# A hybrid decoder layer on one core: the learned tokens' values in one product, and the recurrence's weights rounded behind an eviction

## The chip, the cores and the metric

The kernel runs on one core of a Trainium2 chip. The metric is the device time of one execution in microseconds (us) on the slowest core, which here is the only one. The times are medians of several runs on the chip; the profile shows one further execution.

## The reference, cut to what matters

The layer takes 1024 tokens of width 1024, puts 16 learned tokens ahead of them, and computes a SwiGLU block, a mixer of two parallel head groups, and a second SwiGLU block, all in float32:

```
h = h + 1/2 * swiglu_1(rms_norm(h))
u = rms_norm(h) @ w_in            # one projection for both head groups
o = concat(hgrn2(u_hgrn), stick_breaking(u_sb))
h = h + o @ w_out
h = h + 1/2 * swiglu_2(rms_norm(h))

# recurrence, 4 heads of 128 x 128
S_t = diag(f_t) S_(t-1) + (1 - f_t) v_t^T ;  o_t = S_t^T q_t
# attention, 8 heads of width 64, strictly causal, z = q.k / sqrt(64)
A[t,s] = sigmoid(z_ts) * prod over s<j<t of (1 - sigmoid(z_tj)) ;  o = A v
```

The columns s of A run over the 16 learned tokens too. The change touches the product A v for those 16 columns, and the weights of the recurrence's part of w_in.

## The kernel before, in words

A float32 product on TensorE (PE) is made of three matmuls of rounded parts: each operand is split into an upper part (rounded to the type fp32r, "hi") and a lower part (what is left, "lo"), and hi·hi, lo·hi and hi·lo are added up in a PSUM bank (`product`, L251 to L261; the matmuls are L258, L259 and L260). A column of 128 outputs of w_in takes 24 such matmuls for every piece of up to 512 tokens.

The weights of such a column come through `split_w` (L224). One DMA on the queue of SyncE (SP) loads 128x1024 numbers (`raw`, two buffers, L236). ScalarE (ACT) rounds them (`wh`, a cast, L241), and VectorE (DVE) subtracts (`wl`, L243); `wh` and `wl` have three buffers each.

The first SwiGLU block ends a little before 700 us. Then come the projections of the attention (until about 840 us). For every pair of heads `sb_v` (L1432) brings the values into rows per token: DVE transposes 32x32 blocks (`vt`), ACT and DVE split them (`vhl`), and SP stores them into a buffer in DRAM, vD (L1454), from which a head's values come back as one tile v of 128 rows, 9 groups and 128 columns (64 upper parts, 64 lower parts, L1531). Group 0 holds the 16 learned tokens, in 16 of its 128 rows; the other rows are filled with zeros by 16 DMAs (L1598). The 16 learned tokens' part is handled last in each pair.

The recurrence needs 16 columns of w_in: v, f, q and g for each of its four heads (`hgrn_fill`, L1127). `part` (L1168) makes one half of one piece of a column. A column's first call loads and splits the weights of the column after it. A piece that is finished is emptied from its bank by `use`: for v by one copy on ACT (L1144), for f by two sigmoids on ACT (L1150, L1151) with two products on DVE (L1152, L1155), and for q and g by a sigmoid on ACT (L1158) and a product on DVE (L1159). v and f have four pieces of 256 or 264 tokens, q and g two of 512.

From about 862 to 1142 us a braid runs: PE's order is written out by hand and alternates the attention's jobs with halves of the recurrence's columns. A job takes 256 queries of a head. Scores (`z`, L1649 to L1652, two banks) go through two sigmoids on ACT (keep L1655, sig L1656) that leave the bank free, a running product on DVE (L1659), and a product on GpSimd (POOL, L1665). PE then transposes the weights ("flip", L1504 for four blocks of 128 keys, L1558 for the learned tokens; two banks). `sb_parts` (L1625) splits what was flipped: ACT rounds (L1627), DVE subtracts (L1628), into the tiles wu, or wm for the learned tokens, and the bank is free. PE multiplies with the values (`values`): L1579 takes all 128 columns of v with the upper part of the weights, L1581 the 64 upper columns of v with the lower part. So the learned tokens cost two matmuls per job, each over 128 rows of which 16 hold something.

The instructions of ACT, DVE, GpSimd and SP are put into an order by the framework's scheduler ahead of the run, and each of these engines then takes its instructions strictly in that order. `issue_after` tells the scheduler to place an instruction behind another one.

Of the kernel before, what the change touches and what calls it, by code (L numbers as in the profile page):

```python
# [49 lines left out]
class Block:  # L50
# [172 lines left out]

    def split_w(self, view, parts=None):  # L224
        nc = self.nc
        n = int(np.prod(view.shape[1:]))
        if parts is not None:
            got = []
            for i, tag in enumerate(self.w_tags):
                t = self.wp.tile([P, n], F32R, tag=tag, name="w" + "hl"[i], bufs=self.w_bufs)  # L230
                self.last_load = nc.sync.dma_start(t.bitcast(F32), parts[:, i])
                got.append(t)
            return got
        raw = self.wp.tile([P, n], F32, tag="raw", name="raw", bufs=self.raw_bufs)
        to = raw.rearrange("p (k f) -> p k f", k=view.shape[1]) if len(view.shape) == 3 else raw
        self.last_load = nc.sync.dma_start(to, view)  # L236
        hi = self.wp.tile([P, n], F32R, tag="wh", name="wh", bufs=self.w_bufs)
        if self.split_on_vector:
            nc.vector.tensor_copy(hi, raw)
        else:  # L240
            self.rounded = nc.scalar.copy(hi, raw)  # L241
        lo = self.wp.tile([P, n], F32R, tag="wl", name="wl", bufs=self.w_bufs)
        nc.vector.tensor_sub(lo, raw, hi.bitcast(F32))  # L243
        return hi, lo

    def col_tile(self, w, col):
        return self.split_w(
            w[:, col : col + P].rearrange("(k p) f -> p k f", p=P), self.parted.get(col)
        )
# [877 lines left out]
    def hgrn_fill(self, xh, xl, pool, dst):  # L1127
# [8 lines left out]
        def use(kind, h, ps, c0, n):  # L1136
# [6 lines left out]
            if kind == "v":  # L1143
                nc.scalar.copy(t, ps)  # L1144
                with self.tc.issue_after(self.last_load.ins):
                    nc.sync.dma_start(dst[kind][h, :, s], t)
                return
            elif kind == "f":
                k = staged(n)
                nc.scalar.activation(t, ps, AF.Sigmoid)  # L1150
                nc.scalar.activation(k, ps, AF.Sigmoid, scale=-1.0)  # L1151
                nc.vector.tensor_scalar(  # L1152
# [4 lines left out]
            else:  # L1157
                nc.scalar.activation(t, ps, AF.Sigmoid)  # L1158
                nc.vector.tensor_mul(t, t, ps)  # L1159
# [272 lines left out]
    def sb_v(self, p, vT, mix, vD):  # L1432
# [5 lines left out]
        yield 0, 6000  # L1438
        for c0, nb, m in ((META, 16, 32), (META + 512, 16, 32), (0, 1, META)):
            y = mix.tile([P, nb, 32], F32, tag="vt", name="vt", bufs=2)  # L1440
            nc.vector.transpose(
                y.rearrange("p b d -> p (b d)"), vT[:, c0 : c0 + 32 * nb]
            )
            yield 0, 800
            t = mix.tile([P, nb, 2, 32], F32R, tag="vhl", name="vhl", bufs=2)
# [3 lines left out]
            for b in range(4):  # L1449
                to = vD[p, b // 2, :m, j0 : j0 + nb].rearrange(  # L1450
                    "r j (i b d) -> r (j i) b d", i=2, b=2
                )
                with self.tc.issue_after(self.last_load.ins):
                    nc.sync.dma_start(  # L1454
                        to[:, :, b % 2],
                        t.bitcast(F32)[32 * b : 32 * b + m].rearrange("r j i d -> r (j i) d"),
                    )
            yield 0, 1500

# [47 lines left out]
    def sb_jobs(self, keys, fetch, pool):  # L1507
# [29 lines left out]
        def job(p, hh, qs, ks, v, b0):  # L1537
# [15 lines left out]
            def meta():  # L1553
                wm.extend(kept["wm"][0])
                kept["wm"].reverse()
                ps = self.ptr.tile([META, 2, P], F32, tag="tr", name="flip")
                for bi in range(2):
                    nc.tensor.transpose(ps[:, bi, :], sigs[bi][:, :META], self.ident)  # L1558
                self.sb_parts([t[:META] for t in wm], ps)

# [6 lines left out]
            def values(j):  # L1567
# [10 lines left out]
                end = j == b0 + 2  # L1578
                nc.tensor.matmul(o[:, c], vj, w[0], start=j == 0, stop=False,  # L1579
                                 skip_group_check=True)  # L1580
                nc.tensor.matmul(o[:64, c], vj[:, :64], w[1], start=False, stop=end,  # L1581
                                 skip_group_check=True)
# [7 lines left out]
        kept["wm"] = [[fetch.tile([P, 2, P], F32R, name=f"wm{j}{i}") for i in range(2)]  # L1590
                      for j in range(2)]
        for t in chain(*kept["wm"]):
            nc.vector.memset(t.bitcast(F32), 0.0)
        none = kept["wm"][1][1].rearrange("p b t -> p (b t)").bitcast(F32)[META:]
        for p in range(4):
            for a in range(4):
                to = vD[p, :, 0 if a else META :, a].rearrange("h r c -> r h c")
                nc.sync.dma_start(  # L1598
                    to, none[: to.shape[0]].rearrange("r (h c) -> r h c", h=2)
                )  # L1600
# [806 lines left out]
```

## Time and profile before

| what | before |
|---|---|
| median of 3 runs | 1964.71 us (1962.61 to 1965.23) |
| profiled execution | 1965.29 us |
| its span | 1963.6 us |
| busy: PE, DVE, ACT, POOL | 1928.3, 1391.6, 851.7, 449.8 us |
| granted TensorE clock, whole span | 1.0 |
| braid, 862 to 1142 us: PE, DVE, ACT, POOL busy | 272.69, 200.49, 181.16, 98.11 of 280 us |

Rows of single instructions read: start, duration, engine, line, operation, result <- operands, shape, and in brackets how long the engine had stood idle before it and what ended that. Groups of lines read: busy time, mean duration in ns, idle time before. Matmuls are pipelined: one matmul's duration is longer than the distance to the start of the next.

### The profile page before, as it was taken

The numbers are of one execution on the slowest core, as the hardware profiler recorded it, in microseconds if no ns is written. First come the engines' busy times: TensorE is split into PE (matmuls) and PEld (weight loads), VectorE is DVE, ScalarE is ACT, GpSimd is POOL, SyncE is SP. The second block draws the span as 40 slices with busy tenths as digits, with TensorE's granted clock in tenths as the row PEclk, the third lists the DMA queues.
The fourth block names the chain that finished last, engine by engine and source line by source line (L and its number), as shares of the span: only waits on it lengthen the run. The fifth ranks groups of instructions, "written<-read, shape, count | busy, mean of one in ns | idle before, by whom it ended". The sixth has DMA issues, their size and how long they took to land.

```text
span 1963.6 us, 30437 instructions
## 1 busy us (share of the span) xinstructions
PE 1928.3 (98%) x10704; PEld 1622.0 (83%) x10704; DVE 1391.6 (71%) x2186; ACT 851.7 (43%) x1711; POOL 449.8 (23%) x626
## 2 busy tenths in 40 slices
PE   7999999999999999999999999999999999999999
PEld 6888888888888888888888978887888888888887
DVE  6977777877678665567777766667567777767774
ACT  6523343334444544356666635433132332344443
POOL 3010100001000003133333332210544545430000
PEclk9999999999999999999999999999999999999999
DMA  6356787757965415865454167655544444469473
GB/s 211 93 160 174 245 278 237 235 208 280 372 226 185 136 47 144 194 175 148 126 143 126 57 249 216 171 204 181 195 117 140 126 137 119 134 236 330 146 232 113
DMA packets 381688, 355.56 MB, mean 181 GB/s; under 512 B 129040, under 2 KB 284560, under 8 KB 381536
## 3 DMA queue, kind: packets, MB, share of 16 engines
q1 hardware_dynamic: 359728, 288.98, 48.2%
q0 software_dynamic: 20768, 64.63, 9.5%
q8 instruction: 85, 1.39, 0.3%
q14 instruction: 67, 0.55, 0.1%
q10 hardware_dynamic: 1040, 0.00, 0.0%
HBM read 237.95 MB, written 115.57 MB: 180 GB/s over the span
## 4 chain that ended last, share of the span: by engine, by line
PE 91%; DVE 4%; DMA 2%; ACT 2%; issue 1%; POOL 0%; SPq 0%; ACTq 0%; DVEq 0%; POOLq 0%
PE o L741 21%; PE qb L459 18%; PE qc L459 12%; PE qa L459 12%; PE proj L258 5%; PE proj L260 5%; PE proj L259 5%; PE flip L1504 2%; PE wo L259 1%; PE wo L260 1%; PE wo L258 1%; PE mq L1010 1%; PE oacc L1579 1%; PE oacc L1581 1%; PE z L1649 1%
## 5 line engine op out<-in xcount | busy, mean ns | idle before, releaser
L459 PE MATMUL qb<-T,wh 128*128 128x512 f32 x1056 | 344.5, 390 | 1.3 <-ACT T L318 0.8
L459 PEld LDWEIGHTS qb<-T,wh 128*128 128x128 f32 x1056 | 198.1, 188 | 46.1 <-issue 2.5
L459 PE MATMUL qa<-B,wh 128*128 128x512 f32 x696 | 226.8, 391 | 0.0
L258 PE MATMUL proj<-xh,wh 128*128 128x512 f32 (+2 forms) x640 | 213.4, 333 | 2.4 <-ACT st L1151 1.3
L741 PE MATMUL o<-t,w 128*128 128x512 f32 x924 | 211.8, 390 | 0.5 <-DVE u L552 0.5
L260 PE MATMUL proj<-xl,wh 128*128 128x512 f32 (+2 forms) x640 | 209.8, 328 | 0.8 <-DVE xl L1973 0.8
L259 PE MATMUL proj<-xh,wl 128*128 128x512 f32 (+2 forms) x640 | 209.7, 328 | 0.0
L741 PE MATMUL o<-parts 128*128 128x512 f32 x924 | 209.6, 389 | 0.0
L459 PE MATMUL qb<-T,wl 128*128 128x512 f32 x528 | 205.4, 389 | 0.0
L741 PEld LDWEIGHTS o<-t,w 128*128 128x128 f32 x924 | 172.8, 188 | 37.3 <-issue 0.8
L741 PEld LDWEIGHTS o<-parts 128*128 128x128 f32 x924 | 173.4, 188 | 36.0
L371 DVE TENSOR_TENSOR wl<-s,wh 128x512 fp32r<-128x512 f32 x160 | 165.8, 1036 | 50.8 <-ACT wh L369 49.8
L369 ACT CAST wh<-s 128x512 fp32r<-128x512 f32 x160 | 99.7, 624 | 188.5 <-PE qb L459 142.3
L459 PEld LDWEIGHTS qa<-B,wh 128*128 128x128 f32 x696 | 130.6, 188 | 27.3 <-DVE B L845 0.3
L369 ACT CAST wh<-raw 128x512 fp32r<-128x512 f32 x120 | 74.6, 622 | 147.3 <-PE qc L459 99.0
L459 PE MATMUL qa<-B,wl 128*128 128x512 f32 x348 | 135.4, 389 | 0.0
L258 PEld LDWEIGHTS proj<-xh,wh 128*128 128x128 f32 x640 | 120.6, 188 | 14.5 <-ACT st L1151 2.0
L260 PEld LDWEIGHTS proj<-xl,wh 128*128 128x128 f32 x640 | 120.5, 188 | 12.1 <-DVE xl L1973 1.2
L259 PEld LDWEIGHTS proj<-xh,wl 128*128 128x128 f32 x640 | 120.5, 188 | 9.9
L459 PE MATMUL qc<-T,wh 128*128 128x512 f32 x352 | 117.0, 394 | 0.0
L459 PE MATMUL qc<-B,wh 128*128 128x512 f32 x352 | 115.1, 390 | 2.0 <-DVE u L552 1.2
L459 PEld LDWEIGHTS qb<-T,wl 128*128 128x128 f32 x528 | 99.1, 188 | 20.4
(398 smaller groups left out, 3853.9 us busy)
## 6 DMA issues: line engine op xcount, KB each, us to landing
raw<-in_ffn_w_in_dram SPq DMA_DIRECT2D x176, 256.0 KB, 3.9
raw<-in_ffn_w_out_dram SPq DMA_DIRECT2D x112, 256.0 KB, 4.4
w2in<-both SPq DMA_DIRECT2D x28, 512.0 KB, 3.4
raw<-in_w_in_dram SPq DMA_DIRECT2D x25, 512.0 KB, 5.1
ks<-kD SPq DMA_DIRECT2D x32, 260.0 KB, 4.7
wout<-both SPq DMA_DIRECT2D x16, 512.0 KB, 3.8
wh<-w2in SPq DMA_DIRECT2D x27, 256.0 KB, 3.5
wl<-w2in SPq DMA_DIRECT2D x27, 256.0 KB, 3.6
```

The lines of the kernel that those rows point to most:

```text
L258: nc.tensor.matmul(ps, wh[:, s], xs, start=k == 0, stop=False)
L259: nc.tensor.matmul(ps, wl[:, s], xs, start=False, stop=False)
L260: nc.tensor.matmul(ps, wh[:, s], xl[:, k, c0 : c0 + n], start=False, stop=k == nk - 1)
L369: nc.scalar.copy(hi, src)
L371: self.block_lo = nc.vector.tensor_sub(lo, src, hi.bitcast(F32))
L459: nc.tensor.matmul(ps, a[:, k, :], b[:, k, :], start=start and k == 0 and i == 0, stop=k == 3 and i == 2, skip_group_check=True,)
L741: nc.tensor.matmul(banks[bank][m], y[:, m * P : (m + 1) * P], z, start=start and at == 0 and e == 0, stop=q == nq - 1 and e == 2, skip_gro ...
L1010: nc.tensor.matmul(ps[at : at + 32, at_g, :], self.xm[:, 4 * h + k, :], got[i, h][:, k, :], start=h == 0 and kk == 0, stop=h == 1 and kk = ...
L1504: self.nc.tensor.transpose(ps[:m, j, :], src[:, s0 : s0 + m], self.ident)
L1579: nc.tensor.matmul(o[:, c], vj, w[0], start=j == 0, stop=False, skip_group_check=True)
L1581: nc.tensor.matmul(o[:64, c], vj[:, :64], w[1], start=False, stop=end, skip_group_check=True)
L1649: nc.tensor.matmul(z, q, ks[0][:, s0 : s0 + n], start=True, stop=False)
```

## The change

Two parts.

**One product for the learned tokens.** The lower parts of the weights go to rows 32 to 47 of the same tile wm that has the upper parts in rows 0 to 15, and the value tile's group 0 gets the values' upper parts a second time in the rows 32 to 47. One matmul of 128 rows then adds up hi·hi, hi·lo and lo·hi, where two did before. For this `sb_v` stores the learned tokens' upper parts twice (16 more small DMAs in all), the zeros have other shapes (20 DMAs in place of 16), and wm has two tiles in place of four. In `sb_v` the learned tokens' group comes first in each pair, not last, without the two yields that follow each other group.

**Rounding behind an eviction.** In the recurrence, a column's first call only issues the load. The cast on ACT and the subtraction on DVE are emitted later: behind the eviction of the second piece (v, f) or of the first (q, g), with `issue_after` that eviction. The weights two columns on are no longer fetched in the first column.

```
-    def split_w(self, view, parts=None):
+    def split_w(self, view, parts=None, hold=False):
...
-        hi = self.wp.tile([P, n], F32R, tag="wh", name="wh", bufs=self.w_bufs)
...
+        def split(after=None):
+            hi = self.wp.tile([P, n], F32R, tag="wh", name="wh", bufs=self.w_bufs)
+            with self.tc.issue_after(after) if after else ExitStack():
...
+                    self.rounded = nc.scalar.copy(hi, raw)
+            lo = self.wp.tile([P, n], F32R, tag="wl", name="wl", bufs=self.w_bufs)
+            nc.vector.tensor_sub(lo, raw, hi.bitcast(F32))
+            return hi, lo
+
+        return split if hold else split()
...
-                nc.scalar.copy(t, ps)
+                self.emptied = nc.scalar.copy(t, ps).ins
...
-                nc.scalar.activation(k, ps, AF.Sigmoid, scale=-1.0)
+                self.emptied = nc.scalar.activation(k, ps, AF.Sigmoid, scale=-1.0).ins
...
-                nc.scalar.activation(t, ps, AF.Sigmoid)
+                self.emptied = nc.scalar.activation(t, ps, AF.Sigmoid).ins
...
-                for c in cols[i + 1 : i + (3 if i == 0 else 2)]:
+                for c in cols[i + 1 : i + 2]:
                     if c not in self.ahead_w:
-                        self.ahead_w[c] = self.col_tile(self.a["w_in"][0], c)
+                        self.ahead_w[c] = self.col_tile(self.a["w_in"][0], c, True)
...
+                following = cols[i + 1] if i + 1 < len(plan) else None
+                if ci == (plan[i][0] in "vf") and callable(self.ahead_w.get(following)):
+                    self.ahead_w[following] = self.ahead_w[following](self.emptied)
...
-        for c0, nb, m in ((META, 16, 32), (META + 512, 16, 32), (0, 1, META)):
+        for c0, nb, m in ((0, 1, META), (META, 16, 32), (META + 512, 16, 32)):
...
-            yield 0, 800
+            if c0:
+                yield 0, 800
...
+                if c0 == 0:
+                    with self.tc.issue_after(self.last_load.ins):
+                        nc.sync.dma_start(
+                            vD[p, b // 2, :m, 1, 32 * (b % 2) : 32 * (b % 2) + 32],
+                            t.bitcast(F32)[32 * b : 32 * b + m, 0, 0],
+                        )
...
-            yield 0, 1500
+            if c0:
+                yield 0, 1500
...
-                self.sb_parts([t[:META] for t in wm], ps)
+                self.sb_parts([wm[0][at : at + META] for at in (0, 32)], ps)
...
-                    w = [t.rearrange("p b t -> p (b t)") for t in wm]
-                    vj, c = v[:, 0], slice(0, 256)
+                    w, vj, c = [wm[0].rearrange("p b t -> p (b t)")], v[:, 0], slice(0, 256)
...
-                nc.tensor.matmul(o[:, c], vj, w[0], start=j == 0, stop=False,
+                nc.tensor.matmul(o[:, c], vj, w[0], start=j == 0, stop=end,
                                  skip_group_check=True)
-                nc.tensor.matmul(o[:64, c], vj[:, :64], w[1], start=False, stop=end,
-                                 skip_group_check=True)
-                if end:
+                if not end:
+                    nc.tensor.matmul(o[:64, c], vj[:, :64], w[1], start=False, stop=False,
+                                     skip_group_check=True)
...
-            for a in range(4):
-                to = vD[p, :, 0 if a else META :, a].rearrange("h r c -> r h c")
+            for a, r0, r1, c0 in ((0, META, 32, 0), (1, META, 32, 0), (1, 0, META, 64),
+                                  (2, 0, 32, 0), (3, 0, 32, 0)):
```

Lines behind L224 have moved by up to 16 in the changed kernel: the cast is L244 there, the subtraction L246, the eviction L1163, the split of wu and wm L1643 and L1644, the sigmoids keep and sig L1671 and L1672, the value stores L1464 and L1469.

ACT's queue at the table load ahead of the recurrence's first f column. Before:

```order
L1144 COPY st<-proj 128x256
L1446 CAST vhl<-vt 128x32
L1425 ACTIVATE ohi<-kT,kg 128x528
L241 CAST wh<-raw 128x1024
L1150 ACT_TABLE_LOAD
L1150 ACTIVATE st<-proj 128x264
L1151 ACTIVATE st<-proj 128x264
L1150 ACTIVATE st<-proj 128x264
L1151 ACTIVATE st<-proj 128x264
L1150 ACTIVATE st<-proj 128x256
```

ACT's queue at the same place of the changed kernel:

```order
L1149 COPY st<-proj 128x256
L1433 ACTIVATE ohi<-kT,kg 128x528
L1155 ACT_TABLE_LOAD
L1155 ACTIVATE st<-proj 128x264
L1156 ACTIVATE st<-proj 128x264
L1155 ACTIVATE st<-proj 128x264
L1156 ACTIVATE st<-proj 128x264
L244 CAST wh<-raw 128x1024
L1155 ACTIVATE st<-proj 128x256
```

The cast has moved from ahead of the table load to behind the second piece's sigmoids, and the learned tokens' vhl no longer stands in this piece of the queue.

ACT's queue in the braid, at a first half of a column q or g (983.71 us in the profile of before), before:

```order
L1158 ACTIVATE st<-proj 128x512
L1627 CAST wu<-flip 128x4x128
L1655 ACTIVATE keep<-z 128x392
L1656 ACTIVATE sig<-z 128x392
L1627 CAST wu<-flip 128x4x128
```

ACT's queue there in the changed kernel:

```order
L1163 ACTIVATE st<-proj 128x512
L244 CAST wh<-raw 128x1024
L1643 CAST wu<-flip 128x4x128
L1671 ACTIVATE keep<-z 128x392
L1672 ACTIVATE sig<-z 128x392
L1643 CAST wu<-flip 128x4x128
```

The weights' cast has come between the eviction and the attention's work. DVE's queue at that place, before:

```order
L1159 TENSOR_TENSOR st<-st,proj 128x512
L1628 TENSOR_TENSOR wu<-flip,wu 128x4x128
L1659 SCALAR_TENSOR_TENSOR keep<-keep,idle 128x393
L1628 TENSOR_TENSOR wu<-flip,wu 128x4x128
L1621 TENSOR_TENSOR ot<-oacc,olow 64x256
```

DVE's queue there in the changed kernel:

```order
L1164 TENSOR_TENSOR st<-st,proj 128x512
L246 TENSOR_TENSOR wl<-raw,wh 128x1024
L1644 TENSOR_TENSOR wu<-flip,wu 128x4x128
L1675 SCALAR_TENSOR_TENSOR keep<-keep,idle 128x393
L1644 TENSOR_TENSOR wu<-flip,wu 128x4x128
L1637 TENSOR_TENSOR ot<-oacc,olow 64x256
```

The subtraction wl stands ahead of both wu of this job.

More of the change, by code (lines that the diff above doesn't have):

```diff
@@ L236, in split_w, with col_tile @@
         self.last_load = nc.sync.dma_start(to, view)
-        hi = self.wp.tile([P, n], F32R, tag="wh", name="wh", bufs=self.w_bufs)
[L238 to L246, printed above, removed]
+        def split(after=None):
+            hi = self.wp.tile([P, n], F32R, tag="wh", name="wh", bufs=self.w_bufs)
+            with self.tc.issue_after(after) if after else ExitStack():
+                if self.split_on_vector:
+                    nc.vector.tensor_copy(hi, raw)
+                else:
+                    self.rounded = nc.scalar.copy(hi, raw)
[3 more added lines that the diff above has]
+        return split if hold else split()
+    def col_tile(self, w, col, hold=False):
         return self.split_w(
-            w[:, col : col + P].rearrange("(k p) f -> p k f", p=P), self.parted.get(col)
+            w[:, col : col + P].rearrange("(k p) f -> p k f", p=P), self.parted.get(col), hold
         )
@@ L1553, in meta @@
             def meta():
-                wm.extend(kept["wm"][0])
+                wm.append(kept["wm"][0])
                 kept["wm"].reverse()
@@ L1588, in job @@
             return score, turn, value
-        kept["wm"] = [[fetch.tile([P, 2, P], F32R, name=f"wm{j}{i}") for i in range(2)]
-                      for j in range(2)]
-        for t in chain(*kept["wm"]):
+        kept["wm"] = [fetch.tile([P, 2, P], F32R, name=f"wm{j}") for j in range(2)]
+        for t in kept["wm"]:
             nc.vector.memset(t.bitcast(F32), 0.0)
-        none = kept["wm"][1][1].rearrange("p b t -> p (b t)").bitcast(F32)[META:]
+        none = kept["wm"][1].bitcast(F32)[64:]
         for p in range(4):
-            for a in range(4):
-                to = vD[p, :, 0 if a else META :, a].rearrange("h r c -> r h c")
+            for a, r0, r1, c0 in ((0, META, 32, 0), (1, META, 32, 0), (1, 0, META, 64),
+                                  (2, 0, 32, 0), (3, 0, 32, 0)):
                 nc.sync.dma_start(
-                    to, none[: to.shape[0]].rearrange("r (h c) -> r h c", h=2)
+                    vD[p, :, r0:r1, a, c0:].rearrange("h r c -> r h c"),
+                    none[: r1 - r0, :, c0:],
                 )
```

1 line of the change is left out of this document (added).

## The prediction, as it was put on record

> **What bounds the kernel now.** I read the page's first part, then its chain of work that ended last.
>
> ```profile
> PE 1928.3 (98%) x10704; PEld 1622.0 (83%) x10704; DVE 1391.6 (71%) x2186; ACT 851.7 (43%) x1711; POOL 449.8 (23%) x626
> ...
> PE 91%; DVE 4%; DMA 2%; ACT 2%; issue 1%; POOL 0%; SPq 0%; ACTq 0%; DVEq 0%; POOLq 0%
> ```
>
> TensorE (PE) is busy for 98% of the span and carries 91% of the chain. So two things change the time: matmuls that appear or vanish, and moments at which PE must wait. What ScalarE (ACT), VectorE (DVE) and GpSimd (POOL) do counts only where PE waits for it. The change lies in two stages: the end of the attention's projections, and the braid behind it, where attention jobs and the recurrence's projection columns alternate (about 862 to 1142 us). For the braid I read the view by stretches (PE, PEld, DVE, ACT, POOL, then granted clock, DMA share, GB/s) and the waits that end on PE.
>
> ```profile
> 862.00:1142.00 280.00, 272.69 (x1922) 242.10 (x1922) 200.49 (x325) 181.16 (x463) 98.11 (x140) 1.00 0.44 124
> ```
> ```profile
> PE flip L1504 <- DVE wu L1628: 3.0, 7, 0.7
> ...
> PE flip L1504 <- DVE wm L1628: 1.5, 3, 0.6
> ...
> PE z L1649 <- ACT sig L1656: 1.2, 4, 0.5
> ```
>
> PE is busy 97% here at the full granted clock. It idles little, and mostly for a transposed weight block (wu, wm) that DVE has not finished splitting; then the flip has no free bank. DVE is busy 72% and ACT 65% of the stage, but with bursts: they have slack on average and none at certain points.
>
> **The change part by part.** First the learned tokens' product and the weights' split, in the view by lines (busy, mean ns, idle before).
>
> ```profile
> L1581 PE MATMUL oacc<-wm,v 128*64 128x256 f32 x32 | 9.1, 284 | 0.3 <-DVE wm L1628 0.3
> ...
> L243 DVE TENSOR_TENSOR wl<-raw,wh 128x1024 fp32r<-128x1024 f32 x13 | 17.2, 1323 | 7.1 <-ACT wh L241 6.6 <-DMA ks<-kD 0.2
> L241 ACT CAST wh<-raw 128x1024 fp32r<-128x1024 f32 x13 | 13.8, 1058 | 2.5 <-DMA raw<-in_w_in_dram 2.5
> ```
>
> (1) *32 matmuls vanish.* Each row says 284 ns, but matmuls overlap, so what one costs is the distance of starts:
>
> ```profile
> 1045.57 0.28 PE L1579 MATMUL oacc<-wm,v 128*128 128x256 f32 x1
> 1045.69 0.28 PE L1581 MATMUL oacc<-wm,v 128*64 128x256 f32 x1
> 1045.81 0.31 PE L1649 MATMUL z<-ks,qs 128*128 128x328 f32 x1
> ```
>
> 0.12 us from the removed one to the next. 32 x 0.12 = **-3.8 us**. The weight loads that go with them lie beside matmuls (nothing). The single product now waits for DVE's part of wm as a whole, where its first half used to run ahead by 0.12; that can cost between 0 and 32 x 0.12, but the L1581 row waited only 0.3 in all, so I take 0.
>
> (2) *One cast leaves the front of the table load.* ACT's order ahead of the first sigmoids of the recurrence, and the PE row that waits for it:
>
> ```profile
> 853.54 1.04 ACT L241 CAST wh<-raw 128x1024 fp32r<-128x1024 f32 x1
> 854.60 1.28 ACT L1150 ACT_TABLE_LOAD   x1
> 855.89 0.39 ACT L1150 ACTIVATE st<-proj 128x264 f32<-128x264 f32 x1
> 856.18 0.38 ACT L1151 ACTIVATE st<-proj 128x264 f32<-128x264 f32 x1
> ...
> 856.62 0.39 PE L258 MATMUL proj<-xh,wh 128*128 128x256 f32 x1 [1.32 <-ACT st L1151]
> ```
>
> PE stands 1.32 us for a free bank. In the new order the cast comes behind two evictions of that column; the table load starts 1.04 earlier and PE's wait shrinks to about 0.3: **-1.0 us**. What is late next there is the table load itself.
>
> (3) *The old places of the casts in the braid are vacated.* Three of the 13 splits delayed a wu or wm block far enough to show on PE:
>
> ```profile
> 936.95 0.30 PE L1504 MATMUL flip<-ident,sig 128*128 128x128 f32 x1 [0.67 <-DVE wu L1628]
> ...
> 1021.74 0.52 PE L1504 MATMUL flip<-ident,sig 128*128 128x128 f32 x3 [0.17 <-DVE wu L1628]
> ...
> 1111.26 0.41 PE L1504 MATMUL flip<-ident,sig 128*128 128x128 f32 x2 [0.59 <-DVE wm L1628]
> ```
>
> 0.67 + 0.17 + 0.59 = **-1.4 us** comes back. The other ten showed nothing on PE.
>
> (4) *The new places.* Each cast (1.06 us) now stands directly behind an eviction on ACT and each subtraction wl (1.23 to 1.32 us) behind the eviction's arithmetic on DVE, with the attention's work queued behind. Work in the queue that used to stand there starts that much later. I went through the 13 places; they fall into three kinds. **Scores' bank** (three columns, at 873.76, 895.92 and 963.57):
>
> ```profile
> 895.92 0.60 ACT L1158 ACTIVATE st<-proj 128x512 f32<-128x512 f32 x1 [1.69 <-PE proj L260]
> ...
> 896.68 0.55 ACT L1655 ACTIVATE keep<-z 128x456 f32<-128x456 f32 x1
> 897.13 0.55 ACT L1656 ACTIVATE sig<-z 128x456 f32<-128x456 f32 x1
> ...
> 897.73 0.43 PE L1649 MATMUL z<-ks,qs 128*128 128x348 f32 x1
> ```
>
> There are two score banks, so this z needs the bank that sig (ends 897.68) reads last; PE starts 0.05 behind it. With the cast between L1158 and keep, sig ends 1.06 later and so does PE. Three times 1.06 = +3.2. **Flip's bank** (three columns, at 983.71, 1071.86 and 1138.18; a fourth at 1049.86 has twelve projection matmuls behind it that leave 0.3):
>
> ```profile
> 983.71 0.60 ACT L1158 ACTIVATE st<-proj 128x512 f32<-128x512 f32 x1 [1.45 <-PE proj L260]
> 984.20 0.58 ACT L1627 CAST wu<-flip 128x512 fp32r<-128x512 f32 x1
> ...
> 984.94 0.68 DVE L1628 TENSOR_TENSOR wu<-flip,wu 128x512 fp32r<-128x512 f32 x1
> ...
> 985.68 0.39 PE L1558 MATMUL flip<-ident,sig 128*16 128x128 f32 x2
> ...
> 987.23 0.52 PE L1504 MATMUL flip<-ident,sig 128*128 128x128 f32 x3 [0.69 <-DVE wu L1628]
> ```
>
> The flip at 985.68 starts 0.06 behind the end of the wu at 984.94. In the new order the cast takes 984.20 to 985.26 and wl 985.26 to 986.49, so this wu starts at 986.49: 1.55 late, and PE with it. The flip at 987.23 is then late by the same 1.55, not by more. 3 x 1.55 + 0.3 = +5.0. **Columns v and f** (six): the worst and the best that I found are
>
> ```profile
> 1030.88 0.76 ACT L1627 CAST wu<-flip 128x512 fp32r<-128x512 f32 x2
> ...
> 1031.51 0.89 DVE L1628 TENSOR_TENSOR wu<-flip,wu 128x512 fp32r<-128x512 f32 x2
> ...
> 1032.95 0.60 PE L1504 MATMUL flip<-ident,sig 128*128 128x128 f32 x4
> ...
> 1096.62 0.69 DVE L1628 TENSOR_TENSOR wu<-flip,wu 128x512 fp32r<-128x512 f32 x1 [2.44 <-ACT wu L1627]
> ...
> 1096.78 0.33 PE L258 MATMUL proj<-xh,wh 128*128 128x256 f32 x1
> ...
> 1098.24 0.38 PE L1558 MATMUL flip<-ident,sig 128*16 128x128 f32 x2
> ```
>
> In the first, wu moves behind a wl that ends at about 1033.2, and ends near 1034; PE had 0.55 to spare, so +0.95. In the second, twelve projection matmuls (1096.78 to 1098.24) cover a wu that is about 1.7 later: 0. The other four I take at 0.35, between the two and nearer to the covered one, since PE has such a block behind most evictions: 0.95 + 0 + 1.4 = +2.3. Together 3.2 + 5.0 + 2.3 = **+10.5 us**. The bounds: 0, if everything is covered as in the row of 1096.62, and 13 x 1.55 = 20, if nothing is.
>
> (5) *Value stores.* The learned tokens' stores come first in each pair and there are 16 small ones more on SP's queue (and four more zero writes ahead of the stage). A run of four such stores took
>
> ```profile
> 829.37 2.27 SPq L1454 DMA_DIRECT2D vD<-vhl  x4
> ```
>
> so 0.57 each, about 2.3 us more of queue time per pair, ahead of weight loads that are issued many microseconds before their cast. I take 0; if a load were late by the whole 2.3 in one pair PE would stand for up to that. Two of the four zeroings on DVE go, before the braid: 0.
>
> **Sum:** -3.8 - 1.0 - 1.4 + 10.5 = **+4.3 us** on the profiled execution's 1965.29: 1969.6. The median of the runs shown is 0.58 lower than that execution, so I predict **1969.0** (+0.22%).
>
> **The rivals.** *Covered (faster).* The new places cost as little as most of the old ones. For it speaks a place of the old order where a cast already stood right behind an eviction, with wl next on DVE, and no PE wait followed:
>
> ```profile
> 954.81 1.05 ACT L241 CAST wh<-raw 128x1024 fp32r<-128x1024 f32 x1
> ...
> 955.89 1.23 DVE L243 TENSOR_TENSOR wl<-raw,wh 128x1024 fp32r<-128x1024 f32 x1 [0.39 <-ACT wh L241]
> ```
>
> Against it: in the scores' and flips' kinds PE starts 0.05 us behind the instruction that is pushed back. It decides by whether twelve projection matmuls (2.8 us) stand between the eviction and the next flip or z that needs a bank. With all covered, -6.2: 1958.5; with only the scores' kind paid, -3.0: 1961.7.
>
> *Subtraction beside GpSimd (slower still).* One old wl met a product on GpSimd:
>
> ```profile
> 931.17 1.81 POOL L1665 TENSOR_TENSOR sig<-sig,keep 128x912 f32<-128x912 f32 x1 [2.94 <-DVE keep L1659]
> ...
> 931.92 2.14 DVE L243 TENSOR_TENSOR wl<-raw,wh 128x1024 fp32r<-128x1024 f32 x1 [0.92 <-ACT wh L241]
> ```
>
> It took 2.14 instead of 1.23: it ended 1.08 behind the end of sig, as though it had stood still until then. GpSimd is busy 98.11 of 280 us, so 35% of 13 places, 4 or 5, may meet it at 0.9 each: +4, on top of the forecast: 1973. Against it: evictions come after a block of projection, when GpSimd's product is often done. The Trainium skill, page "SBUF — State Buffer", section "Who interferes with whom", says that a VectorE instruction with two SBUF inputs contends with a GpSimd instruction that reads SBUF, and that the later one blocks fully; the rows above agree (1.06 until sig's end, then 1.08 of work). By that rule the price of a meeting is whatever is left of sig when wl starts.
>
> *Stores in the way.* The 2.3 us on SP delay a weight load or a store of the first column, and PE stands in one or two pairs: +2 to +4 beside the forecast, 1971 to 1973. *The products do not shrink*: if the wait for wm takes back what the 32 matmuls give, the sum is +8: also 1973.
>
> **How the numbers follow.** The forecast's case (new places cost 7 to 13 us, so +1 to +7) gets 0.47; about half of it lies beyond +3.9 us, which is 0.2% and about what a measurement of this kernel can tell from no change. Covered: 0.25, of which 0.19 is faster by over 0.2%. GpSimd meetings 0.16, stores 0.07, products that do not shrink 0.05. Faster 0.19; same 0.06 + 0.24 + 0.04 = 0.34; slower 0.47. The range reaches from all covered, 1958.5, to the sums of the slower rivals, 1974.
>
> **What would show it.** Right: a PE row at the start of the recurrence's first f column that waits about 0.3 instead of 1.32; 32 fewer rows of oacc<-wm; waits of flip for wu and wm that grow from 4.5 us to 8 or more and of z for sig from 1.2 to 4; PE's busy time down by some 3 us in the braid while the stage gets longer by about 5. Wrong: if waits of PE in the braid stay at their old sums, (4) is the step that failed; if the stage from 700 to 862 us changes by more than 1.5 us beyond (2), (5) did.

## The result, and the profile after

| | before | after |
|---|---|---|
| median of 6 runs | 1964.24 us (1961.94 to 1966.23) | 1972.22 us (1971.01 to 1973.24) |
| profiled execution, span | 1965.29, 1963.6 us | 1972.07, 1970.3 us |
| mean granted TensorE clock | 1.0 | 0.998 |

The change makes the kernel slower by 8.0 us: the ratio is 1.0042, 95% interval 1.0029 to 1.0055. The forecast was 1969.0 us, slower by 4.3 us than the median shown then (1964.71). The time lies in the range, in the part of it where the sums of the slower rivals lay too (1971 to 1973), and the loss is nearly twice the one forecast.

The page of the changed kernel, busy times and the chain that ended last:

```profile
PE 1928.1 (98%) x10672; PEld 1620.1 (82%) x10672; DVE 1392.2 (71%) x2184; ACT 850.9 (43%) x1711; POOL 448.3 (23%) x626
...
PE 90%; DVE 5%; ACT 2%; DMA 1%; issue 1%; POOL 1%; DVEq 0%; ACTq 0%; POOLq 0%
```

32 matmuls are gone, but PE is busy for as long as before (1928.1 against 1928.3 us), and the chain has moved a per cent from PE to DVE. The first is odd: 32 matmuls of 0.12 us should have taken 3.8 us off. The view by stretches tells where most of it went (columns as before: PE, PEld, DVE, ACT, POOL busy, then the granted clock, DMA share, GB/s). Of 196 stretches of 10 us these four are the ones below 1.0:

```profile
1070.00:1080.00 10.00, 7.69 (x48) 6.20 (x46) 7.43 (x11) 7.25 (x18) 2.24 (x3) 0.99 0.22 70
1080.00:1090.00 10.00, 9.51 (x48) 8.12 (x49) 5.67 (x10) 4.48 (x13) 5.23 (x8) 0.84 0.28 88
...
1140.00:1150.00 10.00, 8.23 (x44) 6.55 (x43) 5.54 (x19) 4.56 (x10) 1.27 (x2) 0.90 0.16 58
1150.00:1160.00 10.00, 10.00 (x42) 8.07 (x41) 4.38 (x32) 1.45 (x2) 0.91 (x2) 0.93 0.86 304
```

The clock falls twice in the braid, in both cases behind a stretch in which PE was idle for two microseconds (7.69 and 8.23 of 10 busy). The rows at the first fall:

```profile
1078.62 0.30 PE L1520 MATMUL flip<-ident,sig 128*128 128x128 f32 x1 [2.19 <-DVE wu L1644]
...
1081.80 0.63 PE L264 MATMUL proj<-xh,wl 128*128 128x512 f32 x1
1082.22 0.63 PE L265 MATMUL proj<-xl,wh 128*128 128x512 f32 x1
1082.65 0.63 PE L263 MATMUL proj<-xh,wh 128*128 128x512 f32 x1
...
1083.61 0.39 PE L263 MATMUL proj<-xh,wh 128*128 128x512 f32 x1
1083.84 0.40 PE L264 MATMUL proj<-xh,wl 128*128 128x512 f32 x1
```

The starts of like matmuls are 0.43 us apart (1081.80 to 1082.22) and then 0.23 again. The record of the granted clock in the trace has half the clock for 3.41 us, from 1079.81 and from 1148.07 on; the two falls cost 1.3 and 1.5 us. The view over such stretches of 3.41 us, the first with the wait of 2.19 us in it and the second with the fall:

```profile
1076.40:1079.81 3.41, 1.22 (x9) 0.86 (x8) 3.10 (x5) 2.86 (x9) 0.15 (x1) 1.00 0.30 106
1079.81:1083.22 3.41, 2.81 (x10) 2.38 (x10) 2.11 (x5) 1.15 (x3) 3.33 (x4) 0.50 0.64 201
```

The waits of PE from 862 to 1152 us (sum, times, longest), of the changed kernel:

```profile
PE flip L1520 <- DVE wu L1644: 5.8, 8, 2.2
...
PE z L1665 <- ACT sig L1672: 3.4, 6, 1.4
...
PE flip L1574 <- DVE wu L1644: 1.7, 1, 1.7
...
PE oacc L1597 <- DVE wu L1644: 1.1, 2, 0.9
...
PE flip L1520 <- DVE wm L1644: 0.8, 2, 0.6
```

Flips and value products that wait for DVE come to 9.4 us in place of 4.8, scores that wait for sig to 3.4 in place of 1.2. That is the form the prediction gave for its step (4). Two of its places, first the flip's bank (ACT, DVE, PE):

```profile
985.48 1.04 ACT L244 CAST wh<-raw 128x1024 fp32r<-128x1024 f32 x1
...
986.55 1.22 DVE L246 TENSOR_TENSOR wl<-raw,wh 128x1024 fp32r<-128x1024 f32 x1 [0.25 <-ACT wh L244]
987.69 0.68 DVE L1644 TENSOR_TENSOR wu<-flip,wu 128x512 fp32r<-128x512 f32 x1
...
988.43 0.39 PE L1574 MATMUL flip<-ident,sig 128*16 128x128 f32 x2 [1.69 <-DVE wu L1644]
```

then the scores' bank:

```profile
896.20 1.04 ACT L244 CAST wh<-raw 128x1024 fp32r<-128x1024 f32 x1
...
897.73 0.56 ACT L1672 ACTIVATE sig<-z 128x456 f32<-128x456 f32 x1
...
898.35 0.43 PE L1665 MATMUL z<-ks,qs 128*128 128x348 f32 x1 [0.68 <-ACT sig L1672]
```

PE waits 1.69 us where it had come 0.06 behind wu, and 0.68 where it had come 0.05 behind sig.

The table load, where the prediction took off 1.0 us:

```profile
852.29 0.74 ACT L1433 ACTIVATE ohi<-kT,kg 128x528 fp32r<-128x528 f32 x1 [2.78 <-DMA qD<-ohi]
853.05 1.28 ACT L1155 ACT_TABLE_LOAD   x1
...
855.06 0.39 PE L263 MATMUL proj<-xh,wh 128*128 128x256 f32 x1 [1.68 <-ACT st L1156]
```

The cast is gone from there, and PE still waits 1.68 us, more than the 1.32 of before: ACT now waits 2.78 us for the buffer of ohi ahead of the load.

To add this up I paired PE's rows of both traces in their order and followed the difference of their starts from 699 to 1166 us of before. It grows from -1.07 to +7.93, so by 9.0 us; each jump is booked to what stands there.

| term | forecast | in the traces |
|---|---|---|
| (1) 32 matmuls | -3.8 | -4.1 |
| (2) table load and the piece behind it | -1.0 | +0.7 |
| (3) old places vacated | -1.4 | -2.2 |
| (4) new places: scores, flips, v and f | 3.2 + 5.0 + 2.3 | 2.6 + 4.9 + 3.7 |
| clock | - | +2.8 |
| projections' stage | 0 | -0.8 |
| small waits of about 0.1 us, the rest | - | +1.4 |

The profiled executions differ by 6.8 us, since 1.07 us ahead of 699 and another 1.1 behind 1166 went the other way in stages that the change doesn't touch.

### The profile page after: what moved, and what is told of

Read it like the earlier page. It is cut to its first block, busy times and chain, and to the rows that moved or that the text cites. A ratio compares the mean times of both kernels' runs of the same rounds, so it can differ in the third digit from the quotient of the medians.

```text
span 1970.3 us, 30407 instructions
## 1 busy us (share of the span) xinstructions
PE 1928.1 (98%) x10672; PEld 1620.1 (82%) x10672; DVE 1392.2 (71%) x2184; ACT 850.9 (43%) x1711; POOL 448.3 (23%) x626
## 4 chain that ended last, share of the span: by engine, by line
PE 90%; DVE 5%; ACT 2%; DMA 1%; issue 1%; POOL 1%; DVEq 0%; ACTq 0%; POOLq 0%
PE o L746 21%; PE qb L464 18%; PE qa L464 12%; PE qc L464 12%; PE proj L263 5%; PE proj L265 5%; PE proj L264 5%; PE flip L1520 1%; PE wo L263 1%; PE wo L265 1%; PE wo L264 1%; PE mq L1015 1%; PE oacc L1594 1%; PE lvl L1287 1%; PE oacc L1597 1%
```

## The experiments

All twelve were timed in rounds with the kernel before on the same chip, in three groups (medians of before 1964.1, 1964.5 and 1964.4 us). "To before" is the ratio with its 95% interval. Where two variants lie closer than their intervals, I add the growth of PE's paired rows from 699 to 1166 us of before (9.0 us for the changed kernel). That growth is of one profiled execution each.

**1. One product alone** (`e1_products_only`): the casts of the recurrence as before, the rest of the change kept.

```
-                for c in cols[i + 1 : i + 2]:
+                for c in cols[i + 1 : i + (3 if i == 0 else 2)]:
...
-                        self.ahead_w[c] = self.col_tile(self.a["w_in"][0], c, True)
+                        self.ahead_w[c] = self.col_tile(self.a["w_in"][0], c)
```

> The one product for the learned tokens with its stores and its order, without the held rounding (casts and loads as before). Theory A (the whole loss comes from the casts behind the evictions, and the products give what 32 distances of 0.12 us give): 3.8 us below before, perhaps 0.5 more from the projections' stage: -3.5 to -4.5 us, ratio about 0.998; 32 rows of oacc fewer, granted clock 1.0. Rival B (the wait for all of wm, or the 16 more stores on SP's queue, take the gain back): -1 to +2 us. Rival C (the products cost by themselves): +2 us or more.

Measured: 1963.98 us, to before 1.0002 (0.9993 to 1.0011). Rival B: nothing is gained. The clock was 0.999, and the fall was at the table load, as PE's rows show:

```profile
856.03 0.38 PE L263 MATMUL proj<-xh,wh 128*128 128x256 f32 x1 [1.92 <-ACT st L1156]
...
857.06 0.41 PE L263 MATMUL proj<-xh,wh 128*128 128x256 f32 x1
857.27 0.41 PE L264 MATMUL proj<-xh,wl 128*128 128x256 f32 x1
```

A wait of 1.92 in place of 1.32 us, and then 256 columns take 0.21 us from start to start where 0.12 is usual. The order of the values had moved ACT's and DVE's work at this place.

**2. The held rounding alone** (`e2_hold_only`): `sb_v`, wm and `values` from before, `split_w` and `part` from the change.

> The held rounding alone, with two products for the learned tokens and their values' stores as before. Theory A: 11 to 13 us above before (8.0 measured for the whole change, plus the 3.8 that the products give), with granted clock below 1.0 at one or more places and waits of PE in the braid as in the changed kernel. Rival B or C (part of the 8 us comes from the products or the stores): +5 to +9 us.

Measured: 1975.51 us, to before 1.0055 (1.0042 to 1.0068): +11.4 us, theory A. The whole loss comes from the held rounding. Its wait at the first f column was 0.42 us: without the new order of the values, step (2) does give 0.9 of the 1.0 us that the prediction took. But it isn't a gain: where that column ends and the next begins, PE's rows lose 1.4 us again (862.62 to 862.94 in before). There ACT's cast, now among the column's sigmoids, waits 2.60 us for its weights to land.

**3. No held rounding at the two clock falls** (`e3_not_at_flips`).

```
-                        self.ahead_w[c] = self.col_tile(self.a["w_in"][0], c, True)
+                        self.ahead_w[c] = self.col_tile(self.a["w_in"][0], c, i not in (11, 14))
```

> The changed kernel, but the weights that are rounded in two columns (those in which the changed kernel's trace shows the granted clock falling to half, at 1080 and 1148 us) are rounded at the start of the column as before. Theory A with the clock (a long wait of PE costs itself, about 1.6 us, and then some 1.4 us more because the next 3 us run at half the clock): -5 to -6 us from the changed kernel, +2 to +3 on before, granted clock 1.0 throughout. Rival (the clock's fall costs nothing that the waits do not already hold): -3.2 us from the changed kernel. Rival (the delay comes back elsewhere, since the cast must stand somewhere): less than 2 us gained.

Measured: 1969.69 us, to before 1.0033 (1.0021 to 1.0046): 2.5 us gained on the changed kernel by the medians, 3.3 by the paired rows (5.7 in place of 9.0), about half of what theory A gave. In the profiled execution, the fastest of five, the clock was 1.0 throughout, and both long waits had gone. But the casts at the columns' starts made new waits, of which the longest is

```profile
1060.11 0.52 PE L1520 MATMUL flip<-ident,sig 128*128 128x128 f32 x3 [1.37 <-DVE wu L1644]
```

(+1.2 against before; another +0.9 at the flip that stood at 1125.16 in before). My expectation had taken the vacated places as free.

**4. No held rounding at the scores** (`e4_not_at_scores`): the same edit with `i not in (2, 3, 6)`.

> The changed kernel, but in the three columns where the cast delayed the scores' bank (z waits for sig) the rounding stands at the start of the column as before. Theory A: three waits of 0.8 to 0.95 us vanish and nothing else: -2.6 us from the changed kernel, +5.4 on before, with both falls of the granted clock still there. Rival (these waits only move slack, later waits shrink by them): within 1 us of the changed kernel.

Measured: 1974.12 us, to before 1.0053 (1.0040 to 1.0065): 1.9 us more than the changed kernel by the medians and 2.2 by the paired rows (11.2), where theory A had 2.6 less. The three waits for sig did go, and three new ones came, the first of them

```profile
865.98 0.48 PE L1665 MATMUL z<-ks,qs 128*128 128x456 f32 x1 [1.36 <-ACT sig L1672]
```

with another of 0.57 at a z behind it and a third fall of the clock (0.83 from 870 to 880 us). At 948 to 953 us two flips lost another 1.5 us. So it isn't enough to know what a place costs: where the cast goes instead has a price of the same size.

**5. Learned tokens last** (`e5_learned_last`): the changed kernel with the old order of the groups.

```
-        for c0, nb, m in ((0, 1, META), (META, 16, 32), (META + 512, 16, 32)):
+        for c0, nb, m in ((META, 16, 32), (META + 512, 16, 32), (0, 1, META)):
...
-            if c0:
-                yield 0, 800
+            yield 0, 800
```

(and the second yield likewise.)

> The changed kernel, with the learned tokens' group handled last in each pair again, as before. Theory A2 (the new order puts the 128x512 split of the last values ahead of the last norms on ACT and DVE, so that the table load ahead of the first f column comes 0.6 us later against PE): PE's wait at the first f column falls from 1.68 to about 0.8 to 1.1 us, total -0.5 to -1 us against the changed kernel, with both falls of the granted clock still there. Rival (the order is harmless, the raw load beside the stores of qD is the cause): the wait stays at 1.5 or more.

Measured: 1974.79 us, to before 1.0051 (1.0039 to 1.0064): 2.6 us more by the medians, whose intervals overlap, and the same by the paired rows (9.1); no gain in any case. The profiled execution is the fastest of five: it and one other (1972.4 and 1973.4 us) ran at a mean clock of 0.999, the other three (1974.8 to 1977.1) at 0.997. One fall takes 0.0009 off the mean (half of 3.41 us in 1970), so those three had about two falls more, if each was as long. The wait at the first f column fell to 0.35, so the new order is a cause of that wait; but the next piece waited 1.83 us for ACT, and that column's last one some more. The run also gives the price of the clock by chance. The same flip as at 1078.62 above waited exactly as long, and the clock didn't fall:

```profile
1080.74 0.30 PE L1518 MATMUL flip<-ident,sig 128*128 128x128 f32 x1 [2.19 <-DVE wu L1642]
...
1083.09 0.39 PE L263 MATMUL proj<-xh,wh 128*128 128x512 f32 x1
1083.32 0.40 PE L264 MATMUL proj<-xh,wl 128*128 128x512 f32 x1
```

From that flip to the rows at 1110 of before, the changed kernel loses another 1.3 us against before, and this one 0.0. The traces show in what the two differ. Falls of one execution lie whole multiples of 3.413 us apart (68.26 us, which is 20, in the changed kernel; 211.62 us, which is 62, in run 4), so they start on a fixed grid. This execution fell at 1148.48 us; on its grid the wait of 2.19 us lies across the border at 1080.21:

```profile
1076.80:1080.21 3.41, 1.75 (x12) 1.26 (x10) 2.23 (x4) 2.69 (x6) 0.09 (x1) 1.00 0.17 67
1080.21:1083.62 3.41, 2.28 (x15) 1.82 (x16) 3.29 (x8) 2.37 (x7) 1.84 (x2) 1.00 0.64 199
```

PE was idle for 1.66 and 1.13 us of these two windows, against 2.19 us of one window in the changed kernel.

**6. One product, learned tokens last, nothing held** (`e6_products_learned_last`): runs 1 and 5 together.

> One product for the learned tokens, without the held rounding, and with the learned tokens' group last in each pair as before. Theory A2 (alone, the products' 3.8 us were eaten by the order of the groups: a wait of 1.92 in place of 1.32 us at the first f column, and some 3 us at half the clock behind it): granted clock 1.0 throughout, that wait back at about 1.3, and 3 to 4.5 us below before, ratio 0.998. Rival (the products' gain is lost in the braid or by the 16 more stores): within 1.5 us of before.

Measured: 1963.56 us, to before 0.9999 (0.9990 to 1.0008). The wait at the first f column (1.29 us) and the clock (1.0) came out as theory A2 said, and the gain did not: the rival. The 32 matmuls do give 4.1 us between their neighbours, but from 862 to 1141 us 3.4 us of it come back as other waits: 0.7 and 0.6 us at two places, and some 15 times about 0.12, where PE now comes to a flip that much earlier and waits that much longer for wu. The 0.7 stands behind two wl in a row on DVE, the first of them 2.35 us long beside a product on GpSimd: what the prediction's rival "subtraction beside GpSimd" described turns up here. And at the second f piece stands this (SP's queue, ACT, PE):

```profile
855.33 0.42 SPq L1468 DMA_DIRECT2D vD<-vhl  x1
855.79 0.43 SPq L1151 DMA_DIRECT2D hg_v<-st  x1
...
859.36 0.39 ACT L1156 ACTIVATE st<-proj 128x264 f32<-128x264 f32 x1 [3.68 <-DMA hg_v<-st]
...
859.80 0.38 PE L263 MATMUL proj<-xh,wh 128*128 128x256 f32 x1 [1.28 <-ACT st L1156]
```

Eight small stores, in place of four, now stand ahead of the store of hg_v, which frees the buffer that ACT waits for, which empties the bank that PE waits for. That is the rival "stores in the way" of the prediction.

**7. One hold** (`e7_one_hold`): run 6, with only the rounding ahead of the table load held (`i in (1,)`); as in the changed kernel, the weights two columns on are not fetched in the first column.

> As the run with one product and the learned tokens last, and of the held roundings only the one at the first f column (ahead of the table load before). Theory A: that wait of PE falls to about 0.4, so 0.9 us less than without it: 4 to 5.5 us below before. Rival (what the wait loses there comes back at the next pieces, where the next load's cast and the stores' buffers are late, as in the run with the held rounding alone): no gain over the run without it.

Measured: 1964.55 us, to before 1.0000 (0.9991 to 1.0008). The rival: the wait at the table load went from 1.29 to 0.36, and the next piece's from 1.28 to

```profile
859.38 0.39 PE L263 MATMUL proj<-xh,wh 128*128 128x256 f32 x1 [2.42 <-ACT st L1156]
```

with the clock at half behind it. The store of hg_v ended both; an earlier PE only waits longer for it.

**8. Two holds** (`e8_two_holds`): run 6, with the rounding held at the two places of the clock falls alone (`i in (11, 14)`).

> As the run with one product and the learned tokens last, with the held rounding only in the two columns behind which the changed kernel ran at half the clock. Theory A with the clock: two waits of PE of about 2 us each (1.5 to 1.6 more than before) and two falls of the clock of about 1.4 us each, less what two old places cost: +5 to +6 us against the run without holds, +1 to +2 on before, granted clock 0.998. Rival (the clock falls only where other waits have gone before): +3 us against the run without holds, and clock 1.0.

Measured: 1968.77 us, to before 1.0021 (1.0013 to 1.0030): 5.2 us more than run 6. Two of the braid's thirteen held roundings cost nearly half of the 11.4 us that run 2 lost with all of them. That is theory A with the clock, which fell at both places (0.85 from 1070 to 1080 us, 0.83 from 1140 to 1150).

**9. The small stores on GpSimd's queue** (`e9_copies_on_gpsimd`): run 6 with

```
-                        nc.sync.dma_start(
+                        nc.gpsimd.dma_start(
                             vD[p, b // 2, :m, 1, 32 * (b % 2) : 32 * (b % 2) + 32],
```

> As the run with one product and the learned tokens last, without holds, but the 16 additional small stores are issued from GpSimd's queue in place of SP's. Theory D (they held up the store of hg_v on SP, so ACT waited 3.68 us for a buffer and PE 1.28 us for a bank at the second f piece): that wait of PE vanishes or falls under 0.2, and the time is 1 to 1.5 us below the run with the stores on SP, about 2 us below before. Rival (the buffer is late for another reason, the stores of qD and kD on GpSimd's queue are now held up): the wait stays above 1 us, or moves to the first f piece.

Measured: 1961.95 us, to before 0.9986 (0.9977 to 0.9995), so 2.4 us below before: theory D. SP and ACT at the place:

```profile
851.97 0.42 SPq L1151 DMA_DIRECT2D hg_v<-st  x1
...
855.04 0.39 ACT L1156 ACTIVATE st<-proj 128x264 f32<-128x264 f32 x1 [0.72 <-DMA hg_v<-st]
```

ACT waits 0.72 in place of 3.68 us, and PE not at all at that piece. This version is faster than both kernels, though against the one before only by 0.1%.

**10. Halves** (`e10_halves`): the changed kernel with the held weights cut in two; the second half goes behind the column's next eviction.

```
-                    self.rounded = nc.scalar.copy(hi, raw)
+                        self.rounded = nc.scalar.copy(hi[:, c], raw[:, c])
...
-            nc.vector.tensor_sub(lo, raw, hi.bitcast(F32))
+                nc.vector.tensor_sub(lo[:, c], raw[:, c], hi[:, c].bitcast(F32))
...
-                if ci == (plan[i][0] in "vf") and callable(self.ahead_w.get(following)):
+                if ci >= (plan[i][0] in "vf") and callable(self.ahead_w.get(following)):
```

> The changed kernel, with each held rounding cut in two: half of the weights (cast 128x512, subtraction 128x512) behind the eviction as there, the other half behind the next eviction of the column. Theory A with the clock (what counts beyond the work pushed in is that a single wait is long): no wait above 1.5 us, granted clock 1.0 in the braid, waits at the flips 0.8 in place of 1.6 each and at the scores 0.5 in place of 0.85; at the second places about as many short ones: 3 to 5 us below the changed kernel, +3 to +5 on before. Rival (the sum of the work pushed in is what counts, the clock does not): within 1.5 us of the changed kernel.

Measured: 1966.83 us, to before 1.0014 (1.0005 to 1.0023): 5.4 us below the changed kernel, with the clock at 1.0. That is theory A with the clock; the clock's own term was 2.8 us, and the rest is shorter waits. The wait that was 2.19 us is

```profile
1075.78 0.30 PE L1529 MATMUL flip<-ident,sig 128*128 128x128 f32 x1 [1.33 <-DVE wu L1653]
```

and no wait of the braid is longer.

**11. The subtraction on GpSimd** (`e11_wl_on_gpsimd`).

```
-            nc.vector.tensor_sub(lo, raw, hi.bitcast(F32))
+            (nc.gpsimd if after else nc.vector).tensor_sub(lo, raw, hi.bitcast(F32))
```

> The changed kernel, with the subtraction of the held weights on GpSimd in place of DVE; the casts stay behind the evictions on ACT. Theory A (at the flips the delay of 1.6 is the cast and then the subtraction ahead of wu on DVE; at the scores it is the cast alone): waits at the scores as before the edit (0.8 to 0.95), waits at the flips down to about 1.0, no or one fall of the clock: 3 to 5 us below the changed kernel. Rival (GpSimd is slower at it, near 2 us, and delays its product sig, which the flips need): no gain or a loss.

Measured: 1965.08 us, to before 1.0005 (0.9997 to 1.0014): 7.1 us below the changed kernel, more than theory A gave, since waits in the columns v and f shrank too (0.17 in place of 0.82 us at the flip that stood at 1032.95 in before). By line, and the flip of the second place above:

```profile
L246 POOL TENSOR_TENSOR wl<-raw,wh 128x1024 fp32r<-128x1024 f32 x13 | 31.1, 2389 | 31.7 <-ACT wh L244 31.7
```
```profile
986.39 0.39 PE L1574 MATMUL flip<-ident,sig 128*16 128x128 f32 x2 [1.05 <-DVE wu L1644]
```

GpSimd takes 2.39 us where DVE took 1.30 in the mean, and the kernel is faster all the same. The flip's wait falls from 1.69 to 1.05: the cast alone. The scores' waits stay (0.68 for the z that is at 898.35 above), the second long flip falls from 2.19 to 1.34, and the clock stays at 1.0.

**12. Combined** (`e12_combined`): run 9, with the hold and the later fetch of run 7 and `bufs=5` in place of 4 for st.

> One product, learned tokens last, the 16 additional stores on GpSimd's queue, only the rounding ahead of the table load held, and five buffers in place of four for what leaves the recurrence's banks. Sum of the pieces: -0.9 (wait at the table load) and -1.0 to -1.5 (store in the way) against the run with one product and the learned tokens last: 2.5 to 4 us below before, granted clock 1.0. Rival (the pieces of the first f column share one bottleneck, the loads and stores there, and what one wait loses the next gains): 1 us below before or less.

Measured: 1964.02 us, to before 0.9998 (0.9990 to 1.0007). The rival: the wait at the table load is 0.40, and the wait at the end of the f column 2.13 us, with the clock at half behind it. ACT's queue shows what PE waited for:

```profile
861.10 1.04 ACT L244 CAST wh<-raw 128x1024 fp32r<-128x1024 f32 x1 [2.88 <-DMA raw<-in_w_in_dram]
862.53 0.38 ACT L1156 ACTIVATE st<-proj 128x256 f32<-128x256 f32 x1 [0.38 <-DMA hg_k<-st]
```

The held cast waits 2.88 us for its weights, whose load was issued at 854.00, and the sigmoid that empties the bank stands behind it. What was gained at the first piece is lost there. No run separates the hold from the later fetch.

## Why the prediction was right, and where its size was wrong

The sign and the cause were right: run 2 shows that the held rounding loses 11.4 us, and the trace that it loses it where step (4) said. The time was 3.2 us above the forecast, and the loss 8.0 us for 4.3. Of the signs that were named, the flips' waits came (8.3 us for "8 or more") and the scores' nearly (3.4 for 4); the wait at the first f column didn't shrink, and PE's busy time in the braid fell by about 1 and not 3 us, since the falls of the clock stretch its matmuls. The steps answer as follows.

- **Step (4), the new places: right**, 11.2 us in the trace for 10.5. The two kinds that were worked out from rows came out within 0.6 us; v and f cost 3.7 for 2.3, because the column at 942 us cost 1.6 and not 0.35.
- **The missing term is the clock, +2.8 us.** The prediction treated a wait as its own length. A wait of PE of about two microseconds can also halve the granted clock for 3.41 us. In the runs, waits of 1.92, 2.08, 2.13, 2.19, 2.20 and 2.42 us were followed by a fall, and so were 0.40 + 0.94 + 0.44 us within 2.7 us (at 1145 to 1148 us); 1.68, 1.69 and 1.83 us were not, and 2.19 us once was not. Run 10 took the long waits away and run 8 put two of them back. The Trainium skill, page "TensorE: Matmul & The Clock Gate", section "HAM oscillation — how this bites in real kernels", puts the rule as no idle gap of PE beyond about 3.4 us. Here single gaps of 1.92 to 2.42 us were enough, so the measurement decides. The Trainium skill, the same page, part 1, section "What's actually happening", says that the activity is watched over a free-running window of 3.4 us. The traces agree: the falls of an execution lie on a grid of 3.413 us, and the wait of 2.19 us that no fall followed (run 5) is split by it between two windows. On these grids, from 30 us on, every window in which PE was idle for 1.92 us or more was followed by a fall; between 1.0 and 1.8 us there are both (1.49 and 1.77 us with a fall, 1.70 and 1.74 without), so the idle time alone is not the whole rule.
- **Step (2), the table load: wrong in the changed kernel**, +0.7 for -1.0. It failed at "the table load starts 1.04 earlier": measured against PE's rows it starts 0.4 us later (it comes 1.55 us earlier, and PE 1.91). With the hold alone the wait does shrink (0.42 us, run 2), though the 0.9 us are lost again where the next column begins; with the learned tokens' group first, ACT and DVE split 512 columns of values ahead of the last norms, and the wait is 1.92 us without the hold (run 1), 1.68 with it. In the changed kernel a weight load is issued at 849.91, and the two stores of ohi to qD land after 3.4 and 4.4 us in place of 2.7 and 3.2; that this load is what makes ACT wait 2.78 us is only argued from runs 1 and 2, which lack the load there and wait 2.1 and 2.0 us.
- **Step (1): right at the matmuls** (-4.1), **too simple for the stage.** Run 6 shows that 3.4 of the 4.1 us come back as waits in the braid itself.
- **Step (3): right**, -2.2 for -1.4, with 0.3 us at the flip at 913.91 us, which the prediction had not counted.
- **Step (5), the stores: nothing in the changed kernel, but only because of its order.** With the learned tokens last they cost 1.4 us (runs 6 and 9); with them first, the order costs the 0.6 us at the table load. The prediction had kept both apart.

Of the rivals, subtraction beside GpSimd did not come about in the changed kernel: wl's mean was 1.30 us, and of the thirteen in the braid two were long (1.81 and 1.60). "Covered" didn't either; the places where the cast stood behind an eviction at no cost in before were not a sample of the new ones. "The products do not shrink" had a sum of +8, which is the loss that was measured, but by luck: with the casts held, the products do give something (8.0 us of loss with them, 11.4 without, run 2; 9.0 and 10.8 by the paired rows), while with nothing held they give almost nothing (runs 1 and 6).

What stays open: what besides the idle time decides about a fall when a window holds less than 1.9 us of it, and how much of run 5's median, 2.6 us above the changed kernel's, is the falls of the clock in three of its five executions, whose traces were not kept.

## What to carry to other kernels

Where PE is busy for 97% of a stage, read for every moved instruction of ACT and DVE which bank PE will ask for next: what starts within 0.1 us behind its releaser passed on most of a delay or all of it here (1.59 us for a delay of 1.55, 0.84 for 1.06), and what had twelve matmuls ahead of it passed on next to nothing. Cut or move what would make PE wait for two microseconds at one place (halves, or an engine with slack even at twice the duration), since such a wait can cost another 1.3 to 1.5 us through the clock. Ask of an instruction that is moved whether its own data will be there: a cast that waits for its weights holds up everything behind it (run 12). And take a matmul that is removed as a gain only where PE doesn't come to a wait soon behind it.

## What the runs showed of the hardware

The granted clock fell to half for 3.41 us behind waits of PE of 1.9 to 2.4 us; the two falls of the changed kernel cost 1.3 and 1.5 us. The falls of one execution lay on a grid of 3.413 us, and a wait of 2.19 us that lay across a border of it (1.66 us on one side) was not followed by one. A subtraction of 128x1024 float32 numbers took 2.39 us on GpSimd and in most cases 1.23 on VectorE. A wait on ACT for a buffer can come from a DMA queue two steps away: eight small stores ahead of one store on SP made ACT wait 3.68 us, four 0.72.
